# Splitting the first two loads of a sum-of-differences kernel into a 16 KB-packet part and a 48 KB-packet part

## The chip, the cores and the metric

The kernel runs on one core of a Trainium2 chip. The metric is the device time of one execution in microseconds (us), as a median over runs. Beside it stands the "span" of a profile, from the first to the last instruction, some 2 us shorter (83.7 us in the profiled run of the kernel before, whose time was 85.49 us). DVE is the vector engine, ACT the scalar engine, SP the sync engine; SP and ACT each issue DMA transfers on a queue of their own: in the kernel before ACT issues 8.39 MB, which the profile's page has on queue 10, and SP the other 25.17 MB, on queue 1. The page counts both against the same 16 DMA engines.

## The reference

```
x, y: float32 of 1024 x 4096
out = np.sum(np.abs(x - y), axis=-1)      # 1024 sums
```

Two inputs of 16.8 MB each are read once; 4 KB is written.

## The kernel before

Each of 128 partitions holds 8 rows of x (`xa`, `xb`, 4 rows each) and 4 rows of y (`yb`). Rows 0 to 3 of both come in first, x on SP's queue and y on ACT's, ahead of the barrier that opens the program. Rows 4 to 6 of x follow on SP's queue, then rows 4 to 7 of y into the buffers that the subtractions set free, the last row of both in pieces. DVE subtracts in place; ACT takes the absolute value and sums.

```
put(lambda: nc.sync.dma_start(out=xa, in_=xr[:, 0:H, :]).then_inc(s_first, 16), before="RegisterMove")
put(lambda: nc.scalar.dma_start(out=yb, in_=yr[:, 0:H, :]).then_inc(s_first, 16), before="RegisterMove")
put(lambda: nc.sync.dma_start(out=xb[:, 0:H - 1, :], in_=xr[:, H:K - 1, :]).then_inc(s_xb, 16))
for k in range(H - 1):
    put(lambda: nc.sync.wait_ge(s_sub, k + 1))
    put(lambda: nc.sync.dma_start(out=yb[:, k, :], in_=yr[:, H + k, :]).then_inc(s_row[k], 16))
...   # last row in pieces of 1728, 1056, 640, 384, 288 columns
for k in range(H):
    sub(xa[:, k, :], yb[:, k, :], [(s_first, 32)] if k == 0 else [])
    absum(xa[:, k, :], ro[:, k:k + 1], s_act)
sub(xb[:, 0, :], yb[:, 0, :], [(s_xb, 16), (s_row[0], 16)])
...   # rows 5, 6 in halves, row 7 in pieces, closing sums, output
```

H is 4, K is 8; `put` moves an instruction into the opening block, ahead of the named one.

## Time and profile before

| what | value | how to read it |
|---|---|---|
| time | 85.63 us, 85.59 to 85.64 in 3 runs | median |
| DVE, ACT busy | 36.3 us, 31.6 us | under half of the 83.7 us span each |
| both DMA queues | 94.6% of the span | the resource in use throughout |
| first subtraction | 41.39 us | all of the first 16.8 MB has landed |

The lines that carry this stand in the prediction below.

### The profile page before, as it was taken

The page shows a single profiled execution, that of the slowest core. Times are in us where ns is not written, and L with a number is a line of the kernel's source. Part 1 is how long each engine was busy: PE and PEld are TensorE (multiplying, and loading weights), DVE is VectorE, ACT ScalarE, POOL GpSimd, SP SyncE. Part 2 cuts the span into 40 slices and gives each one's busy share as a digit, 9 for nine tenths or more (in the row PEclk, how much of TensorE's full clock was granted, in tenths as well). Part 3 has the DMA queues.
Part 4 walks back from the last instruction along what each step waited for, and adds up shares of the span by engine and source line. Part 5 has one row for each costly group of instructions (what it writes and reads, how often), then busy time and mean ns, then how long its engine had stood idle before and what let it go on. Part 6 is the DMA issues. An engine that isn't in the chain of part 4 may idle for free.

```text
span 83.7 us, 102 instructions
## 1 busy us (share of the span) xinstructions
DVE 36.3 (43%) x16; ACT 31.6 (38%) x27; POOL 0.2 (0%) x4
## 2 busy tenths in 40 slices
DVE  0000000000000000000299999999199898997870
ACT  5000000000000000000000979798880899999960
POOL 0000000000000000000000000000000000000000
DMA  9569999983999999669899988889999999999910
GB/s 501 219 282 501 501 501 501 501 376 157 470 501 501 501 501 438 282 282 501 376 399 634 470 376 376 376 360 438 438 399 462 407 454 377 423 409 410 392 40 2
DMA packets 2449, 33.56 MB, mean 401 GB/s; under 512 B 401, under 2 KB 913, under 8 KB 1681
## 3 DMA queue, kind: packets, MB, share of 16 engines
q1 hardware_dynamic: 2304, 25.17, 71.5%
q10 hardware_dynamic: 144, 8.39, 23.1%
q14 instruction: 1, 0.00, 0.0%
HBM read 33.55 MB, written 0.00 MB: 401 GB/s over the span
## 4 chain that ended last, share of the span: by engine, by line
DMA 68%; DVE 22%; ACT 7%; ACTq 0%; issue 0%
DMA yb_rows<-in_y_dram 68%; DVE xa_rows L122 16%; ACT xb_rows L127 7%; DVE xb_rows L122 5%; DVE ro_sums L158 1%; ACTq L194 0%
## 5 line engine op out<-in xcount | busy, mean ns | idle before, releaser
L122 DVE TENSOR_TENSOR xa_rows<-xa_rows,yb_rows 128x4096 f32<-128x4096 f32 x4 | 17.4, 4420 | 41.4 <-DMA yb_rows<-in_y_dram 41.4
L127 ACT ACTIVATE xa_rows<-xa_rows 128x4096 f32<-128x4096 f32 x4 | 14.5, 3616 | 45.5 <-DVE xa_rows L122 45.5
L122 DVE TENSOR_TENSOR xb_rows<-xb_rows,yb_rows 128x2048 f32<-128x2048 f32 (+5 forms) x9 | 17.9, 2020 | 3.4 <-DMA yb_rows<-in_y_dram 3.3
L127 ACT ACTIVATE xb_rows<-xb_rows 128x2048 f32<-128x2048 f32 (+5 forms) x9 | 15.2, 1686 | 2.9 <-DVE xb_rows L122 2.8
L127 ACT ACTIVATION_READ_ACCUMULATOR xb_rows<-xb_rows 128x1 f32 x9 | 1.7, 186 | 0.0
L127 ACT ACT_TABLE_LOAD x1 | 1.3, 1283 | 0.9 <-PEq L180 0.9
L127 ACT ACTIVATION_READ_ACCUMULATOR xa_rows<-xa_rows 128x1 f32 x4 | 0.7, 186 | 0.0
L156 DVE TENSOR_TENSOR last_piece<-xb_rows,yb_rows 128x288 f32<-128x288 f32 x1 | 0.5, 459 | 0.2 <-DMA yb_rows<-in_y_dram 0.2
L158 DVE TENSOR_REDUCE ro_sums<-last_piece 128x1 f32<-128x292 f32 x1 | 0.5, 457 | 0.1
L150 DVE TENSOR_REDUCE ro_sums<-half_sums 128x2 f32<-128x4 f32 x1 | 0.1, 150 | 0.0
L180 POOL MEMSET const-bfloat16-1.0<- 128x1 bf16 x1 | 0.1, 102 | 0.0
L180 POOL MEMSET const-uint8-127<- 128x1 uint8 x1 | 0.1, 102 | 0.0
L180 POOL MEMSET const-float32-1.0<- 128x1 f32 x1 | 0.1, 99 | 0.0
L180 POOL MEMSET const-float32-0.0<- 128x1 f32 x1 | 0.1, 98 | 0.2 <-issue 0.2
## 6 DMA issues: line engine op xcount, KB each, us to landing
xb_rows<-in_x_dram SPq DMA_DIRECT2D x1, 6144.0 KB, 54.8
yb_rows<-in_y_dram SPq DMA_DIRECT2D x3, 2048.0 KB, 15.3
xb_rows<-in_x_dram SPq DMA_DIRECT2D x1, 864.0 KB, 17.6
yb_rows<-in_y_dram SPq DMA_DIRECT2D x1, 864.0 KB, 15.8
xb_rows<-in_x_dram SPq DMA_DIRECT2D x1, 528.0 KB, 16.7
yb_rows<-in_y_dram SPq DMA_DIRECT2D x1, 528.0 KB, 17.5
xb_rows<-in_x_dram SPq DMA_DIRECT2D x1, 320.0 KB, 17.8
yb_rows<-in_y_dram SPq DMA_DIRECT2D x1, 320.0 KB, 18.1
```

The source lines that it names most:

```text
L122: put(lambda: nc.vector.tensor_sub(out=tx, in0=tx, in1=ty).then_inc(s_sub, 1))
L127: put(lambda: nc.scalar.activation(tx, tx, ABS, accum_out=to).then_inc(sem, 1))
L150: put(lambda: nc.vector.reduce_sum(out=ro[:, K - 3:K - 1], in_=half, axis=AX).then_inc(s_end, 1))
L156: put(lambda: nc.vector.tensor_sub(out=last[:, n_part:n_part + w], in0=tx, in1=ty).then_inc(s_end, 1))
L158: put(lambda: nc.vector.reduce_sum(out=ro[:, K - 1:K], in_=last, axis=AX, apply_absolute_value=True).then_inc(s_end, 1))
L180: nc = _bacc.Bacc("TRN2", target_bir_lowering=False, num_devices=1)
```

## The change

Its intent: let the first transfers begin with short packets and issue everything needed first ahead of the barrier. The wait of the first subtraction goes from 32 to 64, as four transfers now count into one semaphore.

```
-    put(lambda: nc.sync.dma_start(out=xa, in_=xr[:, 0:H, :]).then_inc(s_first, 16), before="RegisterMove")
-    put(lambda: nc.scalar.dma_start(out=yb, in_=yr[:, 0:H, :]).then_inc(s_first, 16), before="RegisterMove")
+    for r in (slice(0, 1), slice(1, H)):
+        put(lambda: nc.sync.dma_start(out=xa[:, r, :], in_=xr[:, r, :]).then_inc(s_first, 16), before="Drain")
+        put(lambda: nc.scalar.dma_start(out=yb[:, r, :], in_=yr[:, r, :]).then_inc(s_first, 16), before="Drain")
...
-        sub(xa[:, k, :], yb[:, k, :], [(s_first, 32)] if k == 0 else [])
+        sub(xa[:, k, :], yb[:, k, :], [(s_first, 64)] if k == 0 else [])
```

## The prediction

> **What bounds the kernel now.** I read the engine and DMA rows of the page first, then the chain of waits, then the opening of the timeline, then DMA shares by window.
>
> ```profile
> span 83.7 us, 102 instructions
> DVE 36.3 (43%) x16; ACT 31.6 (38%) x27; POOL 0.2 (0%) x4
> DMA  9569999983999999669899988889999999999910
> ...
> q1 hardware_dynamic: 2304, 25.17, 71.5%
> q10 hardware_dynamic: 144, 8.39, 23.1%
> ```
>
> No compute engine is busy for half of the span, while the two queues together keep the 16 DMA engines busy for 71.5 + 23.1 = 94.6% of it. 94.6% of 83.7 is 79.2 us. The trace's packet records say the same: the first data packet starts at 1.00 us and the last ends at 80.08, which is 79.1 us with no room in it. The 5s, 6s and the 3 of the DMA row are not pauses. A slice of that row is 2.09 us and a 64 KB packet lasts longer, so each packet is booked where it starts; the next fence shows that.
>
> ```profile
> core 0: us, DVE busy (x) ACT busy (x) POOL busy (x), PEclk, DMA share, GB/s
> 1.00:2.00 1.00, 0.00 (x0) 1.00 (x1) 0.00 (x0) 1.00 3.13 1049
> ...
> 35.00:36.00 1.00, 0.00 (x0) 0.00 (x0) 0.00 (x0) 1.00 2.44 1049
> ...
> 52.00:53.00 1.00, 1.00 (x1) 1.00 (x1) 0.00 (x0) 1.00 0.00 0
> 53.00:54.00 1.00, 1.00 (x1) 0.89 (x2) 0.00 (x0) 1.00 1.81 786
> ```
>
> A window with 1049 GB/s over 1 us is one 64 KB packet started on each of 16 engines (16 x 65,536 B = 1.05 MB), and the share beside it is how long such a packet lasts: 3.13 us for the very first, 2.44 us in mid-stream (the packet records' median is 2.418). 786 GB/s is 16 packets of 48 KB, 1.81 us each. A share of 0.00 only says that no packet began in that microsecond. So the engines run without a break at 65,536 B / 2.418 us x 16 = 434 GB/s. The one loss inside the stream is the first packet: 3.13 - 2.42 = 0.71 us, call it the filling.
>
> ```profile
> 0.00 0.13 issue
> 0.13 41.24 DMA yb_rows<-in_y_dram
> 41.37 0.02 issue
> 41.39 13.11 DVE xa_rows L122 x3
> 54.49 0.02 issue
> 54.51 15.88 DMA yb_rows<-in_y_dram
> 70.39 0.02 issue
> 70.41 4.51 DVE xb_rows L122 x2
> 74.92 0.02 issue
> 74.94 5.51 ACT xb_rows L127 x8
> ```
>
> The chain shows 13.11 us of DVE between two DMA pieces. Taken literally, an earlier DVE start would pay. It would not: the row issued at 54.51 stands behind earlier transfers of the same queue. Its landing at 70.39 is when the stream gets to it, and the stream is never empty. That landing is what sets the end: two half subtractions, then the run of ACT, then the closing sums. To move the end, a change has to move the stream.
>
> ```profile
> 0.00 0.38 SPq L101 DMA_DIRECT2D xa_rows<-in_x_dram  x1
> 0.13 0.36 ACTq L102 DMA_DIRECT2D yb_rows<-in_y_dram  x1
> ...
> 0.91 1.28 ACT L127 ACT_TABLE_LOAD   x1 [0.91 <-PEq L180]
> 0.91 0.33 SPq L103 DMA_DIRECT2D xb_rows<-in_x_dram  x1
> ```
>
> Both first issues are already the first instructions of the span, and the barrier is over at 0.91. The first packet runs at 1.00, one microsecond after the first issue.
>
> [...] after the sixteen first packets of queue 1 come sixteen of queue 10 and so on alternately, each beginning 1 to 5 ns after its predecessor's end. So x and y advance together whatever their packet size. [...] 16 KB rows take 0.611 us (median of 384 records), 48 KB packets 1.815, 64 KB 2.418. From 16 to 64 KB that is 1.807 us for 48 KB, so a constant part of 0.611 - 0.602 = about 0.009 us per packet. [...]
>
> **The change part by part.**
>
> 1. Position. The issues were first on their queues and ahead of the barrier, and remain so. No gain and no cost.
>
> 2. Two more issues, one on SP and one on ACT, each 0.36 to 0.38 us by the timeline. They delay the barrier, so the issue of the second half of x and the ACT table load go from 0.91 to about 1.3 us, or 1.5 if the queues get in each other's way. The DMA engines first need that x half when the first sixteen packets are done, at 40.3 us (the first semaphore record of queue 1); ACT first computes at 45.85. Both have about 39 us to spare: 0 on the path.
>
> 3. Packet sizes. Per DMA engine, 16 packets of 64 KB (8 of x, 8 of y) become 16 of 16 KB and 16 of 48 KB. Before: 16 x 2.418 = 38.69 us. After: 16 x 0.611 + 16 x 1.815 = 9.78 + 29.04 = 38.82 us. That is +0.13 us on the stream, all on the path.
>
> 4. Semaphore writes. Each transfer ends with one 4-byte record per engine, 9 ns. Two more per engine: +0.02 us.
>
> 5. The wait. The first subtraction waited for 32 and now waits for 64, that is for all four transfers, so row 0 is not used when it lands at about 11 us (1.0 + 0.7 + 16 x 0.611 = 11.5 at the latest). The first subtraction stays at 41.4 + 0.15, about 41.5 us. Even an earlier one would free a y buffer for a transfer that has to queue: now the y row is issued at 45.85, and the stream reaches it only when the three rows of x are through, near 54.8 us (first semaphore record after them). The spare 9 us is not touched.
>
> 6. The filling. I take it as a latency that the first packet pays whatever its size: 0.71 us again, so that the first 16 KB packet lasts about 0.61 + 0.71 = 1.32 us. No change.
>
> 7. The end. From the landing at 70.39 on everything follows as before, with the same pieces.
>
> Sum: +0.13 + 0.02 = +0.15 us, 85.63 + 0.15 = 85.78 us.
>
> **The rivals.** (a) The filling shrinks with the packet. [...] a quarter packet costs 0.71 / 4 = 0.18 us, a saving of 0.53: 85.63 + 0.15 - 0.53 = 85.25 us. For it: only the first packet ever shows the extra time, and the change looks made for this. Against it: the sixteen first packets differ among themselves, 2.89 to 3.44 us for equal sizes, which looks like a latency with a queue behind it. I give it one chance in five. (b) Row 0 feeds DVE early and the whole kernel moves up. Against it: the 64 in the wait; and the stream, saturated from 1.0 to 80.1 us, would not end earlier. It would give 85.6 at best; I give it almost nothing. (c) The new issues collide. Four issues now go out at once from two queues, and [...] engines could idle early, since a 16 KB packet covers only 0.6 us where a 64 KB one covered 2.4. Later pairs on SP show 0.43 to 0.46 us per issue, so up to 0.4 us lost: about 86.15. Against it: after x row 0 each engine has 8 packets, 4.9 us of work, and the y issue starts 0.13 us after the first. One in ten. (d) 16 KB rows read at a stride of eight rows run slower at the start than as whole 64 KB blocks. Against it: rows 4 to 6 of y have that shape already and run at 0.611 us.
>
> **Range and chances.** The sum says 85.78; one fifth of rival (a) pulls by about -0.1, one tenth of rival (c) by +0.04. I predict 85.7 us, range 85.3 to 86.0, which holds (a) nearly whole and misses only a bad (c). Two per cent is 1.71 us, more than any of these terms and more than all of the filling plus the microsecond before the first packet (0.71 + 1.00 = 1.71, just that). Within 2%: 0.98. Faster: 0.01. Slower: 0.01.
>
> **What would show it.** In the changed profile: span about 83.85; four issues on SP and ACT, the barrier's end and the x half's issue near 1.3 to 1.5 us; first packet still at 1.0 us; the opening 16 KB packets about 1.3 us for the first of each engine (rival (a): 0.8) and 0.61 after; the first subtraction at 41.4 to 41.6; queue shares that sum to 79.3 us or so; the y landing of the chain at 70.5 in place of 70.39. Wrong would be: a first subtraction near 11 us, a first packet later than 1.2 us, gaps between the packets of the first 10 us, or a landing at 70.39 that moves by more than half a microsecond.

The sum came to +0.13 us for the packets and +0.02 us for the semaphore writes, 85.78 us in all.

## More of the kernel before

The timeline of the kernel before: start, duration, engine, instruction, and in brackets how long the engine had been idle before it and for what.

```profile
60.70 4.42 DVE L122 TENSOR_TENSOR xb_rows<-xb_rows,yb_rows 128x4096 f32<-128x4096 f32 x1 [1.88 <-DMA yb_rows<-in_y_dram]
```

This is the subtraction of row 4. DVE had been idle for 1.88 us when it began.

## The result, and the profile after

| kernel | median us | runs | lowest to highest |
|---|---|---|---|
| before | 85.61 | 6 | 85.49 to 85.70 |
| changed | 85.55 | 6 | 85.31 to 85.72 |

The ratio is 0.9994, with a 95% interval of 0.9974 to 1.0015: no difference can be told. Ratios in this document are the mean time of one kernel's fast runs over that of the other's of the same rounds, so they are not quite the ratio of the medians that are quoted. The profiled run of the changed kernel was its fastest, 85.31 us, so tenths read from that one profile have to be taken with care.

The page of the changed kernel: engines, DMA row, queues.

```profile
span 83.5 us, 104 instructions
DVE 36.3 (44%) x16; ACT 31.6 (38%) x27; POOL 0.2 (0%) x4
...
q1 hardware_dynamic: 2448, 25.17, 71.5%
q10 hardware_dynamic: 288, 8.39, 23.3%
```

The picture is the one of before: 288 packets in place of 144 on queue 10, and the same 94.8% of the span in DMA. The chain of waits of the changed kernel (start, duration, what):

```profile
0.53 42.29 DMA yb_rows<-in_y_dram
42.82 0.02 issue
42.84 13.11 DVE xa_rows L123 x3
...
55.96 14.26 DMA yb_rows<-in_y_dram
...
70.25 4.50 DVE xb_rows L123 x2
...
74.77 5.50 ACT xb_rows L128 x8
```

From the end of the second DMA piece on everything stands 0.16 to 0.18 us earlier than before (70.25 against 70.41). But the first subtraction starts at 42.84 us and not at 41.39: 1.45 us later. The place where this is swallowed is the subtraction of row 4 in the timeline of the changed kernel:

```profile
60.53 4.43 DVE L123 TENSOR_TENSOR xb_rows<-xb_rows,yb_rows 128x4096 f32<-128x4096 f32 x1 [0.26 <-DMA yb_rows<-in_y_dram]
```

DVE now waits 0.26 us where it waited 1.88. So the change moved something by nine times the 0.16 us by which the end moved, and only the wait behind it kept that out of the result.

The opening, in windows of half a microsecond of the changed kernel (second last column: mean share of the DMA engines, booked where a packet starts; last: GB/s, booked likewise):

```profile
core 0: us, DVE busy (x) ACT busy (x) POOL busy (x), PEclk, DMA share, GB/s
1.00:1.50 0.50, 0.00 (x0) 0.10 (x1) 0.00 (x0) 1.00 1.62 393
...
2.50:3.00 0.50, 0.00 (x0) 0.18 (x1) 0.00 (x0) 1.00 1.21 492
```

393 GB/s over 0.5 us are twelve packets of 16 KB; a share of 1.62 over 0.5 us of 16 engines is 12.96 us for twelve, 1.08 us each. In the second window it is fifteen packets at 0.65 us, nearly the steady 0.61. So the extra time of the start is smaller than before, and it is spread over more than one packet: by the packet records the first packet of each engine lasts 1.00 us on average, 0.39 more than 0.61, and the later ones have the rest. To compare kernels I add it up over all data packets that start in the first 6 us: each one's recorded duration less the median of its size (0.611 us for 16 KB), divided by 16 engines. I call this sum the filling, as the prediction does. It is 0.71 us before and 0.47 after. It does not count when an engine's first packet starts; that comes back below.

### The profile page after: what moved, and what is told of

It is laid out like the page before. It is cut to its first block, busy times and chain, and to the rows that moved or that the text cites. A ratio compares the mean times of both kernels' runs of the same rounds, so it can differ in the third digit from the quotient of the medians.

```text
span 83.5 us, 104 instructions
## 1 busy us (share of the span) xinstructions
DVE 36.3 (44%) x16; ACT 31.6 (38%) x27; POOL 0.2 (0%) x4
## 4 chain that ended last, share of the span: by engine, by line
DMA 68%; DVE 22%; ACT 7%; ACTq 1%; issue 0%
DMA yb_rows<-in_y_dram 68%; DVE xa_rows L123 16%; ACT xb_rows L128 7%; DVE xb_rows L123 5%; DVE ro_sums L159 1%; ACTq L195 0%; ACTq L103 0%
## 5 line engine op out<-in xcount | busy, mean ns | idle before, releaser
L123 DVE TENSOR_TENSOR xa_rows<-xa_rows,yb_rows 128x4096 f32<-128x4096 f32 x4 | 17.4, 4421 | 42.8 <-DMA yb_rows<-in_y_dram 42.8
```

Of the source, the lines that this page charges most:

```text
L123: put(lambda: nc.vector.tensor_sub(out=tx, in0=tx, in1=ty).then_inc(s_sub, 1))
```

## The experiments

Twelve kernels were run, all timed in five rounds beside the kernel before, and all gave the right result. "Packet records" are the trace's list of DMA packets with start, duration, size and queue; they do not name the DMA engine.

| run | median us | ratio to before (95%) | first subtraction us | filling us |
|---|---|---|---|---|
| e1 whole transfers, new position | 85.53 | 1.0002 (0.9976 to 1.0028) | 41.34 | 0.76 |
| e2 rows 1 to 3 after the barrier | 85.37 | 0.9991 (0.9962 to 1.0020) | 42.89 | 0.50 |
| e3 48 KB packets first | 85.57 | 0.9999 (0.9975 to 1.0024) | 41.59 | 0.70 |
| e4 8 KB packets | 88.95 | 1.0397 (1.0373 to 1.0421) | 47.41 | 0.58 |
| e5 row 0 used early | 85.43 | 0.9998 (0.9980 to 1.0016) | 13.82 | 0.45 |
| e6 8 KB packets, wait per row | 86.59 | 1.0124 (1.0110 to 1.0138) | 13.45 | 0.81 |
| e7 all four on one queue | 85.73 | 1.0029 (1.0007 to 1.0050) | 41.28 | 0.68 |
| e8 4 KB packets first | 85.49 | 0.9999 (0.9986 to 1.0012) | 41.34 | 0.47 |
| e9 before, 2.29 us of DVE put in | 85.63 | 1.0004 (0.9991 to 1.0017) | 43.89 | 0.77 |
| e10 changed, 2.29 us put in | 86.81 | 1.0146 (1.0132 to 1.0161) | 45.21 | 0.45 |
| e11 before, 4.43 us put in | 87.42 | 1.0217 (1.0203 to 1.0231) | 45.92 | 0.81 |
| e12 changed, 4.42 us put in | 88.91 | 1.0393 (1.0378 to 1.0408) | 47.33 | 0.44 |

The median of the kernel before was 85.55, 85.51 and 85.55 us in the three groups (e1 to e4, e5 to e8, e9 to e12).

### e1: position alone

```
-    put(... xa, xr[:, 0:H, :] ..., before="RegisterMove")     # and y likewise
+    put(... xa, xr[:, 0:H, :] ..., before="Drain")
```

> Position alone: the two first transfers unsplit, put ahead of the barrier by the new rule. The program comes out instruction for instruction as the kernel before, so this is a measure of noise. Every theory: ratio 1.000, within 0.2%, first sixteen packets 64 KB and about 3.13 us long, first subtraction at 41.4 us. If the time differs by more than 0.3%, differences of that size between other kernels mean nothing.

Measured: ratio 1.0002, first packets 3.17 us on average, first subtraction at 41.34 us. The built program is instruction for instruction that of the kernel before. Part 1 of the prediction, that the new position is no change, is settled. The interval is as wide as 0.26% to either side, so differences of two tenths of a microsecond between kernels are below what these runs can tell.

### e2: rows 1 to 3 behind the barrier

```
-    for r in (slice(0, 1), slice(1, H)):
+    for r, spot in ((slice(0, 1), "Drain"), (slice(1, H), "UnconditionalBranch")):
     ...   # before=spot
```

> Rows 1 to 3 are issued after the barrier, row 0 before it. Theory (the stream is saturated; the four issues crowded together make some first packets start as late as 1.75 us in place of 1.38): first packets start between 1.0 and 1.4 us again, the time is 0.0 to 0.2 us below the changed kernel's, about 85.4 us. Rival (the crowding costs nothing, the spread of starts comes with 16 KB packets or with chance): starts up to 1.7 us as in the changed kernel and the same time.

Measured: 85.37 us, ratio 0.9991. First packets started between 0.99 and 1.44 us, against 0.99 to 1.75 in the changed kernel, but the last data packet of the stream ended at 79.87 us in both profiles. The starts also vary for one and the same opening: up to 1.74, 1.52 and 1.57 us in e5, e10 and e12, which have the changed kernel's. So four issues ahead of the barrier cost nothing that shows, and putting two of them behind it wins nothing that shows.

### e3: the large packets first

```
-    for r in (slice(0, 1), slice(1, H)):
+    for r in (slice(0, H - 1), slice(H - 1, H)):
```

> Rows 0 to 2 first (48 KB packets), then row 3 (16 KB): the same packets and the same number of them, only the order turned. Theory (the extra time of the first packet grows with its size: 0.39 us at 16 KB, 0.71 at 64 KB): 0.6 us extra at 48 KB, so the first packet lasts about 2.4 us, and the time is 0.1 to 0.3 us above the changed kernel's, about 85.75 us. Rival (extra time is a latency, and the changed kernel's smaller value was chance): 0.4 us extra and the same time as the changed kernel.

Measured: the first packets lasted 2.51 us, 0.70 more than the 1.815 of later ones, and the filling was 0.70 us. The theory had said 0.6 for it, the rival 0.4. Its time, 85.57 us, cannot be told from that of any kernel here but e4, e6 and e10 to e12. First subtraction: 41.59 us. The delay of the changed kernel comes from the short packets in front, not from having four transfers.

### e4: 8 KB packets throughout

```
+    W = C // 2                                  # xf, xd, yf, yd: rows 0 to 3 as one run per partition
+    for i in range(2 * H):
+        r = slice(i * W, (i + 1) * W)
+        put(lambda: nc.sync.dma_start(out=xf[:, r], in_=xd[:, r]).then_inc(s_first, 16), before="Drain")
+        put(lambda: nc.scalar.dma_start(out=yf[:, r], in_=yd[:, r]).then_inc(s_first, 16), before="Drain")
     ...   # and the first subtraction waits for 256
```

> The suspected cost multiplied: the same 16.8 MB in 8 KB packets, eight issues a queue ahead of the barrier. Theory (0.009 us per packet lies on the path, since the stream is saturated): 128 packets a DMA engine at 0.310 us are 39.7 us against 38.7 for sixteen of 64 KB, 14 more semaphore records of 0.009 make 0.1, the smaller filling gives back 0.2 to 0.4: about 86.4 us, between 86.1 and 86.8. Rival (packet cost hides in parallel work or in slack): 85.6 us or less.

Measured: 88.95 us, far outside both. An 8 KB packet took 0.309 us, as computed, and the stream's last data packet ended at 80.85 us, 0.77 later than in the kernel before. That part of the theory holds. But the time grew by 3.4 us. The chain of waits of e4 shows where:

```profile
47.41 14.00 DVE xa_rows L127 x4
61.41 3.34 issue
64.76 4.43 DVE xb_rows L127
69.19 0.02 issue
69.21 13.88 ACT xb_rows L132 x13
```

The first subtraction begins at 47.41 us, and from there to the end the chain never returns to a DMA: DVE and ACT have become the bound (the four subtractions of whole rows last 17.4 us together, so the 3.34 us of "issue" are the last of them, still running). Why so late? The packet records of e4 show, after 40.4 us, an 8 KB packet of y and a 48 KB packet of x's second half in turn:

```
start us   queue, bytes
40.110     y  8192
40.420     x     4
40.426     y  8192
40.739     x 49152
42.551     y  8192
42.857     x 49152
44.672     y  8192
44.980     x 49152
46.797     y     4
```

(Each start here is within 4 ns of the end of the record above it, as in a chain on one DMA engine; which engine it was the records do not say. The records of 4 bytes I take for the ones that raise the semaphore, and call them semaphore records: there are 16 per transfer, as many as a wait counts for one, and the first subtraction started 0.47 to 0.60 us after the last of y's: 47.41 against 46.94 us here, 41.39 against 40.79 before, 42.84 against 42.34 changed.) By the time y's first packet started, x had put through 3.9 packets per DMA engine. In these records turns go by packet, so x reached its second half that many packets ahead, and each remaining 8 KB of y (0.31 us) then waited for 48 KB of x (1.81 us, 40.739 to 42.551). The last y data packet ended at 45.13 us, the last semaphore record of y came at 46.94.

The changed kernel shows the same in small. Per DMA engine, two 16 KB packets of x went out before the first of y (one 64 KB packet in the kernel before). The last y data packet ended at 40.53 us, even earlier than the 40.79 of before. But the 4-byte semaphore records of y came at 42.06 to 42.34 us: each stood behind one 48 KB packet of x, 1.815 us. In the kernel before they came at 40.29 to 40.79 us, directly behind the data. One such chain of each:

```
before                     changed
37.852     y 65536         38.433     x     4
40.280     x     4         38.439     y 49152
40.286     y     4         40.250     x 49152
40.292     x 49152         42.062     y     4
```

Why x was two packets ahead is seen in the starts: in every kernel with two queues and first packets of 16 KB or less (changed, e2, e4, e5, e6, e8, e10, e12) y's first packet started at 2.63 to 2.89 us, though y was issued at 0.12 or 0.13. Up to then x ran alone: two packets of 16 KB per engine, 3.9 of 8 KB. A first packet of 64 KB lasts past that time (3.13 us from 1.0 us on; y started at 3.98 us in the kernel before), so there x is one ahead. Why y's queue took that long, no run here shows. What the records do show is that the queues took turns by packet (before, in the opening: 16 packets of 64 KB of x, 16 of y, and so on), and that a semaphore record waited for its turn as data did (changed: y's at 42.062 us, at the end of the 48 KB packet of x from 40.250).

### e5: row 0 used as soon as it lands

```
+    for r, sem in ((slice(0, 1), s_zero), (slice(1, H), s_first)):
     ...   # .then_inc(sem, 16)
-        sub(..., [(s_first, 64)] if k == 0 else [])
+        sub(..., [(s_zero, 32)] if k == 0 else [(s_first, 32)] if k == 1 else [])
```

> The changed kernel, but the first subtraction waits for the two 16 KB transfers alone (semaphore of their own), the second for the rest. Theory (the saturated stream sets the end, the subtractions have 9 us to spare): the first subtraction starts near 13.6 us in place of 42.84, the other three near 42.8 to 42.9, the row of y that needs its buffer lands as before, the time is the changed kernel's within 0.2 us: about 85.5. Rival (the start of the subtractions is on the path, as the chain of waits has it): 4.4 us of subtraction are taken out, and the time falls by 1 us or more.

Measured: 85.43 us, ratio 0.9998. In the timeline of e5 (idle time in brackets):

```profile
13.82 4.42 DVE L124 TENSOR_TENSOR xa_rows<-xa_rows,yb_rows 128x4096 f32<-128x4096 f32 x1 [13.82 <-DMA yb_rows<-in_y_dram]
...
60.58 4.43 DVE L124 TENSOR_TENSOR xb_rows<-xb_rows,yb_rows 128x4096 f32<-128x4096 f32 x1 [4.59 <-DMA yb_rows<-in_y_dram]
```

A subtraction of 4.42 us was taken out of the stretch from 42.8 us on, and the wait of row 4 grew from 0.26 to 4.59 us, nearly by that. Row 4 still starts at 60.6. What the stream delivers sets the end, as the theory has it; the rival falls.

### e6: 8 KB packets with a wait per row

```
-        ... .then_inc(s_first, 16) ...          # of e4
+        ... .then_inc(s_up[i // 2], 16) ...
-        sub(..., [(s_first, 256)] if k == 0 else [])
+        sub(..., [(s_up[k], 64)])
```

> The 8 KB packets again, with a wait per row in place of one for everything. Theory (of the 3.4 us of the 8 KB run, the packets and semaphore records cost 0.8 us of stream, whose last packet ended at 80.85 in place of 80.08; the rest came because the last y landing was 47.4 us and used up the spare time): subtractions start near 13 us and follow the rows, DVE is waiting for DMA again at the end, the stream ends near 80.9, the time is 86.2 to 86.6. Rival (the 3.4 us are packet cost or the eight issues themselves): 88.5 us or more again.

Measured: 86.59 us, inside the theory's range. In the timeline of e6 the subtraction of row 4 waits for DMA again:

```profile
61.87 4.42 DVE L127 TENSOR_TENSOR xb_rows<-xb_rows,yb_rows 128x4096 f32<-128x4096 f32 x1 [9.63 <-DMA yb_rows<-in_y_dram]
```

e4 and e6 have the same transfers and differ in the waits only. Of the 3.4 us of e4, 88.95 - 86.59 = 2.4 come from the late start of the subtractions; the remaining 86.59 - 85.51 = 1.1 us belong to the stream, which ended at 81.24 us in this profile (80.9 had been expected).

### e7: one queue in place of two

```
-        put(lambda: nc.scalar.dma_start(out=yb[:, r, :], ...
+        put(lambda: nc.sync.dma_start(out=yb[:, r, :], ...
```

> The changed kernel with all four first transfers issued by SP in the order x0, y0, x1 to 3, y1 to 3; ACT issues none. Theory (in the changed kernel the y data had landed at 40.5 us and only the 4-byte semaphore records stood behind 48 KB packets of the second half of x, because x had two packets' start and the queues take turns by packet): with one queue there are no turns, so the first subtraction starts at 41.0 to 41.4 us in place of 42.84. The time stays at 85.3 to 85.7, since 1.5 us are within the spare time. Rival (y lands later because of its rows of 48 KB themselves): 42.8 us again.

Measured: first subtraction at 41.28 us, as the theory said, with the same 16 KB and 48 KB rows. Without a second queue nothing overtakes y, and the 1.5 us of delay are gone. The time was 85.73 us, ratio 1.0029 with an interval that excludes 1 by a little (1.0007 to 1.0050), so slightly slower; the expected upper end was 85.7, so the time narrowly missed its range; why is open. Its filling was 0.68 us although its first packets have 16 KB.

### e8: 4 KB packets first

```
-    for r in (slice(0, 1), slice(1, H)):        # rows
+    for r in (slice(0, 1024), slice(1024, H * C)):   # columns of rows 0 to 3 as one run
```

> First transfers of 4 KB packets, then 60 KB ones, ahead of the barrier. Theory (the filling is mostly a latency that small first packets show in more than one packet: 0.71 us in all at 64 KB, 0.70 at 48, 0.47 at 16, 0.58 at 8): 0.4 to 0.6 us in all, and a time within 0.2 us of the changed kernel's, 85.3 to 85.7. Rival (the filling is in proportion to the packet, so at 4 KB nearly nothing is left): 0.1 us, and a time 0.4 us below the changed kernel's, about 85.1.

Measured: filling 0.47 us, ratio 0.9999. In proportion to the packet it would be 0.71 x 4 / 64 = 0.04 us, so the rival falls. The first subtraction is back at 41.34 us. The records show why: x's eight 4 KB packets per engine were through by 3.4 us and y's eight by 4.5 us. x's 60 KB packets began only at 4.15 to 4.49 us, behind y's last 4 KB, and from there both queues went on with 60 KB packets in strict turns, x one packet ahead as in the kernel before.

### e9 to e12: how much delay is free?

The changed kernel lost 1.45 us at the first subtraction and paid nothing. Was it close to paying? Before the first subtraction DVE gets work that changes no value:

```
+    put(lambda: nc.vector.wait_ge(s_first, 32))          # 64 in the changed kernel
+    put(lambda: nc.vector.tensor_tensor(out=xa[:, 3, 0:w], in0=xa[:, 3, 0:w], in1=xa[:, 3, 0:w],
+                                        op=mybir.AluOpType.max).then_inc(s_pad, 1))
-        sub(..., [(s_first, 32)] if k == 0 else [])
+        sub(..., [(s_pad, 1)] if k == 0 else [])         # w = 2048 (e9, e10) or 4096 (e11, e12)
```

The semaphore `s_pad` makes the first subtraction wait for the added instruction.

> The kernel before with 2.29 us of DVE work put in ahead of the first subtraction (the maximum of half a row with itself, which changes no value). It moves the first subtraction from 41.39 to about 43.7 us, as a late y landing would, and leaves the stream alone. Theory (the subtractions of the kernel before can start late by what DVE later waits for DMA: 1.88 us ahead of row 4, then 0.40, 0.40, 0.42, 0.24 and 0.20, 3.5 us in all): no change, 85.5 to 85.7 us. Rival (9 us to spare, as the prediction had it): no change either. Rival (none to spare): 87.8 us.

> The changed kernel with the same 2.29 us put in. Theory (its first subtraction is already 1.45 us late, so that only 0.26 us are left ahead of row 4, and with 0.40, 0.40, 0.42, 0.23 and 0.17 some 1.9 in all): 0.3 to 0.6 us slower, about 86.0 us. Rival (9 us to spare): 85.5 us.

> The kernel before with 4.42 us of DVE work put in (a whole row). Theory: 4.4 less the 3.5 to spare, 0.9 us slower, about 86.4 us. Rival (9 us to spare): 85.5 us.

> The changed kernel with 4.42 us put in. Theory: 4.4 less the 1.9 to spare, 2.5 us slower, about 88.0 us, and so 1.6 us slower than the kernel before with the same work, though without it the two are equal. Rival (9 us to spare): 85.5 us.

Measured: 85.63, 86.81, 87.42 and 88.91 us against 85.55. The kernel before takes the 2.29 us for nothing; of 4.43 us it passes on 87.42 - 85.55 = 1.87, so about 2.6 us are free. The changed kernel passes on 1.26 of 2.29 and 3.36 of 4.42, so about 1.0 us is free, by both runs. The difference, 1.5 us, is the delay of its first subtraction (1.45). Both rivals, "9 us to spare" and "none", fall. The chain of waits of e9 (first two lines) still goes through the DMA near its end; that of e10 (last two) does not:

```profile
57.01 13.58 DMA yb_rows<-in_y_dram
70.61 4.50 DVE xb_rows L123 x2
...
62.56 4.43 DVE xb_rows L124
67.01 13.88 ACT xb_rows L129 x13
```

The theory's own numbers were 0.8 to 1.0 us too low in e10 to e12. It had added up DVE's waits, 3.5 and 1.9 us. The waits of e12 show what it left out (who waited for whom, us in total, times, longest):

```profile
DVE ro_sums L162 <- ACT xb_rows L129: 1.8, 1, 1.8
```

In e12, where all rows come late, ACT, which follows DVE with one instruction of delay, closes the kernel, and DVE's last sum waits 1.8 us for it. The room that DVE has near the end is not room for ACT.

## Why the prediction was right or wrong

The time was right: 85.55 us measured, 85.7 predicted, within 2% as said, and no term of more than three tenths on the stream. The main reason holds: the stream of packets is without gaps and sets the end (e5: taking 4.4 us of subtraction out of the way gains nothing). But that the time came out right was in part luck: the change delayed the first subtraction by 1.45 us, which was not foreseen, and this fitted into a room that was less than a third of the 9 us counted on.

By the steps of the prediction:

1. Position: right, the same program (e1).
2. Two more issues off the path: right. The ACT table load and the issue of x's second half went from 0.91 to 1.40 us, within the 1.3 to 1.5 predicted.
3. Packet sizes, +0.13 us: right in sign, about twice too large. 16 KB packets took 0.612 us and 48 KB packets 1.815 in the changed kernel, as reckoned. But the prediction read the records as each beginning "1 to 5 ns after its predecessor's end"; they begin 1 to 4 ns before it. Sixteen more packets, each overlapping by some 4 ns, bring the cost down to about +0.07. With 8 KB packets the cost grew to 0.8 to 1.2 us of stream (e4, e6), where the same reckoning had given about 0.9 net.
4. Semaphore writes, +0.02 us: right in duration, 9 ns each (they start 6 ns apart). It was wrong to see them as duration only. Where they stand in the queue matters far more: behind one 48 KB packet, 1.815 us.
5. The wait: this step failed. It said "The first subtraction stays at 41.4 + 0.15, about 41.5 us" and "The spare 9 us is not touched." It started at 42.84, because x was two packets ahead of y at the start in place of one, and y's semaphore records then stood behind a 48 KB packet each (e4 magnifies it, e7 and e8 remove it). And the room was not 9 us: that is how early the transfer of row 4 is issued. What counts for the end is how late DVE and ACT can begin and still keep up, and that was 2.6 us (e9, e11). The change used 1.5 of them; 1.0 is left (e10, e12). Row 0 was to land at "11.5 at the latest"; its y part came at 13.06 us or later, for the same reason. The prediction had concluded from the records that "x and y advance together whatever their packet size"; by packets they nearly do, by bytes they do not once one is ahead and the sizes differ (e4: turns of 8 KB of y and 48 KB of x).
6. The filling, "0.71 us again": too large. The unsplit opening shows 0.71 to 0.81 us in four profiles (before, e1, e9, e11), the changed one 0.44 to 0.50 in five (changed, e2, e5, e10, e12), so about 0.3 us are won. The first packet lasted 1.00 us, neither the 1.32 of the prediction nor the 0.8 of rival (a). Rival (a), which had it in proportion, overstated the gain: it gave 0.18 at 16 KB, and e8 shows 0.47 at 4 KB. What does set it is open: e7 has 16 KB packets and 0.68 us, and two profiles of the same 8 KB opening show 0.58 and 0.81. Nor is all of the 0.3 won: the mean start of an engine's first packet, which the filling leaves out, went from 1.10 to 1.14 us in the four to 1.22 to 1.27 (1.17 in e2), about 0.1 later.
7. The end: right; from the landing of row 6 of y (70.2 us) on, the same pieces follow.

With the measured terms the sum on the stream is +0.07 + 0.01 - 0.3 + 0.1, or about -0.1 us: 85.5. The records show the same gain directly: the mean start of x's second half, behind the whole of the first, is 40.51 to 40.56 us in the four unsplit profiles and 40.39 to 40.47 in the five with the changed opening. That agrees with the 85.55, but the times cannot show so small a gain (0.9994, interval 0.9974 to 1.0015), and it stays an estimate from the packet records. Rival (b), row 0 early, was tested by e5 and gained nothing that shows. Rival (c), the collision of issues by up to 0.4 us (86.18 by the prediction's own terms, not 86.15), shows at most as the 0.1 us of later starts: no other order or place of the four issues (e2, e3, e7) changed the time by more than 0.3%. Rival (d), slow 16 KB rows at the start, falls: from 3 us on the 16 KB packets of the opening took 0.611 us.

No version among the twelve beats the kernel before by more than the noise.

## What to carry to other kernels

Here a gapless DMA stream, 94.6% of the span, set the end. Cutting its transfers differently moved the time by what that added or saved on the stream itself (1.1 us in e6, whose stream ended at 81.24 us in place of 80.08), as long as the landings stayed within the room of the engines behind it, 2.6 us in the kernel before. But it moved single landings by microseconds: the first subtraction by 1.45 us in the changed kernel, by 6.0 in e4, where the room was used up and the time grew by 3.4 us. The two queues took turns by packet in these records (e4: 0.31 us for 8 KB of y, then 1.81 us for 48 KB of x): with two queues, ask how many packets one is ahead and how large the packets are that it then puts between the other's last ones, and remember that the completion signal waited for its turn too, 1.815 us in the changed kernel. "The time did not change" does not mean "nothing changed": look at the waits just behind the changed place, and measure the room that is left by putting known work in.
